# Four-layer decoder trunk: q, k and v of an attention head projected with time on partitions, and a scheduler with other durations

## The chip, the cores and the metric

The kernel runs on one core of a Trainium2 chip. The metric is device time in microseconds (us) of one execution. The kernel before was run three times: 1918.64, 1926.33 and 1927.67 us, a median of 1926.33. Its profile is of one further execution.

A core has five engines that matter here, each with a queue that it works through in order: TensorE (PE in the profile; its weight loads are PEld), VectorE (DVE), ScalarE (ACT), GpSimd (POOL) and SyncE (SP), which here only issues DMA transfers.

## The reference

x is 512 steps of time by D = 1024 channels. Four layers, each `x + Mixer(RMSNorm(x))`, with the mixers A, B, C, A; the inner width is E = 2048.

```python
def conformer_conv_mixer(h, ...):                     # A: layers 0 and 3
    val, glu_gate, z = jnp.split(h @ w_in, 3, axis=-1)
    u = causal_depthwise_conv(val * jax.nn.sigmoid(glu_gate), conv_w) + conv_b   # 31 taps
    u = jax.nn.silu(layer_norm(u, ln_g, ln_b))
    return (u * jax.nn.silu(z)) @ w_out

def forgetting_attention_mixer(h, ...):               # B: layer 1; 16 heads of 128 channels
    q, k, v, z, f_logit = jnp.split(h @ w_in, [E, 2 * E, 3 * E, 4 * E], axis=-1)
    q = rms_norm(q, q_norm_g); k = rms_norm(k, k_norm_g)        # per head
    c = jnp.cumsum(jax.nn.log_sigmoid(f_logit + f_bias), axis=1)
    # logits = q k^T / sqrt(128) + c[t] - c[s] for s <= t, softmax, times v
    o = blocked_forgetting_attention(q, k, v, c)
    return (o * jax.nn.silu(z)) @ w_out

def short_conv_mixer(h, ...):                         # C: layer 2
    u, b_gate, c_gate, z = jnp.split(h @ w_in, 4, axis=-1)
    return (b_gate * causal_depthwise_conv(c_gate * u, conv_w) * jax.nn.silu(z)) @ w_out
```

All of it is float32.

## The kernel before, in words

**Matrix products.** Channels lie on the 128 partitions and the 512 steps of time along the columns. Every operand of a product is cut into two parts of the type fp32r, `hi` (a cast) and `lo` (the rest, by a subtraction), and a product is three: hi·hi, hi·lo and lo·hi. The weights come in chunks of 128 x 1024 (512 KB) by DMA from SP into a ring of three places, `w_raw`; ACT casts a chunk to `w_hi` (L309), POOL or DVE makes `w_lo` (L407), each in a ring of four. One chunk gives 24 matmuls: 8 tiles of d, three products, 512 columns each (`project`). So each use of a chunk needs, in this order, its DMA, its cast on ACT and its subtraction.

**The order.** The code lists all operations in the order of the computation. `Plan.trace` then deals them out: it keeps an estimated duration for each operation and engine, and lets each engine that is free by these estimates take the first operation in the list whose operands are there. An operand counts as there LATENCY = 0.13 us after the end of the operation that made it. The chip never sees the estimates. It sees each engine's order, and semaphores for what must be waited for. A wrong estimate therefore gives an order in which an engine waits at one instruction while others behind it could run.

**A conformer layer.** The in-projection (val, gate, z) and the 31 taps run together, taps on DVE and POOL (a few tiles on PE). Then the layer norm, and sixteen tiles g, each made by DVE and ACT from a tile `d` and cut into `g_hi` (ACT, L309) and `g_lo` (DVE or POOL, L360). The out-projection (`out_projection`) takes them for 384 matmuls: accumulators o0 to o3 take two tiles g at a time, a pair with one chunk (24 matmuls, 8 pairs, 192 in all); o4 to o7 need all sixteen g and take two chunks each (48 matmuls each).

**Attention.** After f (the forget gates) there are sixteen heads. In each, q, k, v and z are projected by one chunk each into a bank of PSUM, channels on partitions, and multiplied by the layer's `rstd` on DVE (`take`, L324). The norms of q and k are over partitions: the squares are cut in two parts and summed by matmuls with a matrix of ones (`qs`, `ks`), and 1/sqrt is worked out on 128 x 512 (`rsqrt`). v is transposed on PE (`vt`). Logits `lg` for four blocks of 128 query steps have 128 to 512 columns; DVE adds the forget gates (`ct`, and `nc` from DMA) and the mask, ACT takes the exponential, DVE divides by `rsum`. The probabilities are transposed (`pt`, in the one bank `tr`), cut in two parts, and multiplied with v into `op`. In the second half of the heads their z·op products are cut into g as in a conformer layer, and the out-projection is the same.

PSUM has eight banks: three `mm`, two `acc`, and one each of `tr`, `sum` and `o`. A bank is taken again only when all that read it are done.

**Layer 2** has the same kind of projections without heads; its order comes from the same planner.

## Time and profile before

| | us |
|---|---|
| three runs | 1918.64, 1926.33, 1927.67 |
| span of the profiled execution, first to last instruction | 1925.0 |
| PE busy | 1789.5 |
| DVE busy | 1306.4 |
| POOL busy | 1030.9 |
| ACT busy | 903.1 |

The page gives no time of the profiled execution apart from its span, which lies 1.3 us under the median of the runs. The page cuts the span into 40 slices, of 48 us each:

```profile
PE   6999997799999998989999999999999899999789
DVE  7999999826777767687724344444412899989851
PEclk9999998899999999999999999999999999999889
```

The first row is PE's busy share in tenths, the second that of DVE, the third the TensorE clock that was granted. Layer 0 takes slices 1 to 9, attention 10 to 21 or so, layer 2 up to slice 31, and layer 3 the rest. The dips of PE stand near the end of the layers 0 and 3, together with dips of the clock.

### The profile page before, as it was taken

The page shows a single profiled execution, that of the slowest core. Times are in us where ns is not written, and L with a number is a line of the kernel's source. Part 1 is how long each engine was busy: PE and PEld are TensorE (multiplying, and loading weights), DVE is VectorE, ACT ScalarE, POOL GpSimd, SP SyncE. Part 2 cuts the span into 40 slices and gives each one's busy share as a digit, 9 for nine tenths or more (in the row PEclk, how much of TensorE's full clock was granted, in tenths as well). Part 3 has the DMA queues.
Part 4 walks back from the last instruction along what each step waited for, and adds up shares of the span by engine and source line. Part 5 has one row for each costly group of instructions (what it writes and reads, how often), then busy time and mean ns, then how long its engine had stood idle before and what let it go on. Part 6 is the DMA issues. An engine that isn't in the chain of part 4 may idle for free. (4 is left out here: it accounts for less than half of the span.)

```text
span 1925.0 us, 21354 instructions
## 1 busy us (share of the span) xinstructions
PE 1789.5 (93%) x7952; PEld 1454.9 (76%) x7952; DVE 1306.4 (68%) x1829; ACT 903.1 (47%) x1335; POOL 1030.9 (54%) x598
## 2 busy tenths in 40 slices
PE   6999997799999998989999999999999899999789
PEld 4788885587787777767778788888888677878567
DVE  7999999826777767687724344444412899989851
ACT  5567864335565555555523222222223456775531
POOL 6899785544344333443435332323334599967652
PEclk9999998899999999999999999999999999999889
DMA  4233321122322221212122223232322232322112
GB/s 165 98 122 101 124 93 55 55 88 89 105 82 83 71 73 64 83 44 66 66 77 92 94 93 105 88 109 88 103 95 88 88 132 88 113 96 88 58 63 77
DMA packets 51831, 171.36 MB, mean 89 GB/s; under 512 B 5888, under 2 KB 5888, under 8 KB 51728
## 3 DMA queue, kind: packets, MB, share of 16 engines
q1 hardware_dynamic: 51728, 170.01, 26.2%
q8 instruction: 62, 1.02, 0.2%
q14 instruction: 41, 0.34, 0.1%
HBM read 167.86 MB, written 2.13 MB: 88 GB/s over the span
## 5 line engine op out<-in xcount | busy, mean ns | idle before, releaser
L407 POOL TENSOR_TENSOR w_lo<-w_raw,w_hi 128x1024 fp32r<-128x1024 f32 x244 | 597.3, 2454 | 722.3 <-PE z L373 227.4
L309 ACT CAST w_hi<-w_raw 128x1024 fp32r<-128x1024 f32 x289 | 302.7, 1051 | 550.1 <-PE z L373 169.4
L335 DVE SCALAR_TENSOR_TENSOR cv<-u,vt,cv 128x487 f32<-128x487 f32 (+25 forms) x710 | 464.5, 728 | 2.0
L373 PE MATMUL o<-g_hi,w_hi 128*128 128x512 f32 x512 | 136.3, 409 | 43.8 <-ACT g_hi L309 23.1
L324 DVE TENSOR_TENSOR x<-o,x 128x512 f32<-128x512 f32 x32 | 20.9, 686 | 212.3 <-PE o L373 212.3
L373 PEld LDWEIGHTS o<-g_hi,w_hi 128*128 128x128 f32 x512 | 100.7, 198 | 68.2 <-ACT g_hi L309 24.6
L373 PE MATMUL o<-g_lo,w_hi 128*128 128x512 f32 x512 | 129.8, 395 | 5.9 <-DVE g_lo L360 5.9
L373 PE MATMUL o<-g_hi,w_lo 128*128 128x512 f32 x512 | 128.9, 393 | 0.0
L324 POOL TENSOR_TENSOR pacc<-prod,pacc 128x508 f32<-128x508 f32 (+3 forms) x104 | 124.5, 1202 | 7.9 <-ACT prod L311 5.5
L373 PEld LDWEIGHTS o<-g_lo,w_hi 128*128 128x128 f32 x512 | 97.2, 191 | 28.1 <-DVE g_lo L360 7.7
L373 PEld LDWEIGHTS o<-g_hi,w_lo 128*128 128x128 f32 x512 | 97.0, 190 | 20.3
L407 DVE TENSOR_TENSOR w_lo<-w_raw,w_hi 128x1024 fp32r<-128x1024 f32 x45 | 78.9, 1758 | 18.9 <-PE u L373 17.7
L243 ACT ACT_TABLE_LOAD x69 | 88.5, 1283 | 1.2
L311 ACT ACTIVATE prod<-u,vt 128x510 f32<-128x510 f32 (+4 forms) x124 | 79.8, 710 | 15.5 <-DVE u L324 15.4
L324 DVE TENSOR_TENSOR z<-z,rstd 128x512 f32<-128x512 f32 x32 | 22.1, 692 | 92.2 <-PE z L373 92.2
L373 PE MATMUL z<-hl,w_hi 128*128 128x512 f32 x256 | 73.0, 433 | 0.0
L373 PE MATMUL z<-hn_hi,w_hi 128*128 128x512 f32 x256 | 66.6, 405 | 5.1 <-ACT sz L311 4.5
L373 PE MATMUL val<-hn_hi,w_hi 128*128 128x512 f32 x224 | 58.2, 399 | 11.9 <-ACT hn_hi L309 6.1
L373 PE MATMUL z<-hh,w_lo 128*128 128x512 f32 x256 | 65.9, 400 | 3.4 <-DVE w_lo L407 3.4
L373 PE MATMUL z<-hn_hi,w_lo 128*128 128x512 f32 x256 | 64.5, 395 | 0.0
L373 PE MATMUL z<-hn_lo,w_hi 128*128 128x512 f32 x256 | 64.5, 395 | 0.0
L373 PE MATMUL z<-hh,w_hi 128*128 128x512 f32 x256 | 63.6, 391 | 0.8 <-DVE u L324 0.8
(247 smaller groups left out, 3902.6 us busy)
## 6 DMA issues: line engine op xcount, KB each, us to landing
w_raw<-w SPq DMA_DIRECT2D x289, 512.0 KB, 3.6
pw<-pw SPq DMA_DIRECT2D x36, 256.0 KB, 4.4
nc<-cd SPq DMA_DIRECT2D x16, 256.0 KB, 4.1
x<-x SPq DMA_DIRECT2D x8, 256.0 KB, 5.5
out<-x SPq DMA_DIRECT2D x8, 256.0 KB, 2.2
vt<-vec SPq DMA_DIRECT2D x1, 577.5 KB, 4.6
cd<-nc SPq DMA_DIRECT2D x1, 32.0 KB, 1.6
vt<-vec SPq DMA_DIRECT2D x1, 16.0 KB, 1.7
```

What stands on the lines that cost most here:

```text
L243: switch(table)
L309: nc.scalar.copy(of(dst, d), of(src, s))
L311: nc.scalar.activation(of(dst, d), of(src, s), func, **kw)
L324: eng[e].tensor_tensor(of(dst, d), of(a, s), of(b, sb), op)
L335: nc.vector.scalar_tensor_tensor(of(dst, d), of(a, s), c, bb.bitcast(F32) if b_f32r else bb, op0, op1)
L373: nc.tensor.matmul(o, a, b, start=start, stop=stop)
L407: eng[e].tensor_tensor(lo(), raw(), hi().bitcast(F32), A.subtract)
```

## The change

**1. Attention's projections.** For a head, q, k and v are computed together with time on the partitions. The stationary operand is a block of 128 time steps of the layer's input (`hh` or `hl`), the moving one holds the weights of q, k and v side by side, 384 columns. Four banks (three `mm` and `sum`) take the four blocks of time. The weights come in a new array `wq`, four chunks of 128 x 768 (384 KB) for a head, each with two tiles of d. That makes 96 matmuls of 384 columns a head. z keeps its form (`gate`) and goes to the bank `o`; `op` goes to `acc`. f has an array of its own, `wf`, with a chunk of 240 columns.

The norms are now sums along a row: ACT squares a block, DVE adds up the 128 columns of q and of k into a 128 x 8 tile, and 1/sqrt is worked out on 128 x 8. v is scaled straight out of the bank by ACT (`vh`) and DVE (`vl`), without a transpose; q and k are scaled on DVE (`qk`) and then transposed on PE (`across`, eight transposes a head). The layer's own 1/sqrt is needed per row as well (`norm_tokens`: eight small matmuls).

```diff
-        def take(h, name):
-            acc, f = psum("mm", f"{name}{h}"), slot(f"{name}{h}")
-            project(acc, h_)
-            tt(("dve",), f, acc, st.rstd, A.mult, boost=-200)
-            return f
-        def normalise(f, h, name, g):
-            sq = slot("sq")
-            act(sq, f, AF.Square)
-            sp = split(sq, "sq", ("dve", "pool"))
-            ms = psum("sum", f"{name}s{h}")
-            sums(ms, ones_hr, sp)
-            stt(f, f, g, rsqrt(ms, "r"), A.mult, A.mult)
-            return split(f, f"{name}{h}", ("dve", "pool"))
+        def tokens(h):
+            banks = [psum("mm" if b < 3 else "sum", f"qkv{h}_{b}") for b in range(NB)]
+            for c in range(ND // 2):
+                hi, lo = chunk()
+                for b in range(NB):
+                    ks = (2 * c, 2 * c + 1)
+                    mms(lambda b=b, ks=ks, hi=hi, lo=lo: [
+                            (banks[b]()[:, : 3 * HD], a[k]()[:, blk(b)],
+                             w()[:, (k - ks[0]) * 3 * HD : (k - ks[0] + 1) * 3 * HD],
+                             k == 0 and g == 0, k == ND - 1 and g == 2)
+                            for k in ks for g, (a, w) in enumerate(
+                                ((st.hh, hi), (st.hl, hi), (st.hh, lo)))],
+                        [banks[b]], 6 * pe_time(3 * HD),
+                        [hi, lo, *(a[k] for k in ks for a in (st.hh, st.hl))])
+            ssq, r, nt, rr = norms[h % 2]
+            for b in range(NB):
+                sq, s = slot("sq"), slice(0, 2 * HD)
+                act(sq, banks[b], AF.Square, s=s)
+                plan.op({"dve": dve_time(2 * HD)}, lambda e, b=b, sq=sq, s=s: nc.vector.tensor_reduce(
+                    ssq()[:, 2 * b : 2 * b + 2], sq()[:, s].rearrange("p (a c) -> p a c", c=HD),
+                    mybir.AxisListType.X, A.add), [sq], [ssq])
+            vh, vl = slot(f"vh{h}", F32R), slot(f"vl{h}", F32R)
+            for b in range(NB):
...
+            tt(("dve",), ssq, ssq, rt2, A.mult, s=n8)
+            rsqrt(ssq, None, bufs=(r, nt), s=n8)
+            tt(("dve",), rr, r, rt, A.mult, s=n8)
...
+                plan.op({"dve": dve_time(2 * HD)}, scale, [banks[b], rr], [qk[b // 2]])
+            return qk, vh, vl
+        def gate(h):
+            zp, z = psum("o", f"z{h}"), slot(f"z{h}")
+            project(zp, h_)
+            tt(("dve",), z, zp, st.rstd, A.mult)
+            act(z, z, AF.Silu)
+            return z
```

**2. Smaller edits in attention.** The mask is an `affine_select` on POOL in place of an addition on DVE. The `lo` parts of weights and of g are made by DVE alone in this layer.

```diff
-        lo_engines["now"] = ("pool", "dve")
+        lo_engines["now"] = ("dve",)
...
-                plan.op({"dve": 0.2}, lambda e, i=i: nc.vector.tensor_tensor(
-                    p[i]()[:, blk(i)], p[i]()[:, blk(i)], mask(), A.add), [p[i], mask], [p[i]])
+                plan.op({"pool": 0.3}, lambda e, i=i: nc.gpsimd.affine_select(
...
-            op = psum("o", f"op{h}")
+            op = psum("acc", f"op{h}")
...
-            gh[k], gl[k] = split(gs[k], f"g{layer}_{k}", ("dve", "pool"))
+            gh[k], gl[k] = split(gs[k], f"g{layer}_{k}", ("dve",))
```

**3. The planner's durations, for all layers.** They are set nearer to a trace, and an operand made by TensorE for another engine, or by another engine than one's own, counts as there later:

```diff
-    LATENCY = 0.13
+    LATENCY = 0.15
+    SLACK = 0.9
...
-                p.ready = max(p.ready, end + self.LATENCY)
+                late = 0.0
+                if len(p.engines) > 1 or e not in p.engines:
+                    late = self.LATENCY + (self.SLACK if "pe" in p.engines else 0.0)
+                p.ready = max(p.ready, end + late)
...
-        return 0.07 + n * (0.52e-3 if fast else 1.042e-3)
+        return 0.16 + n * (0.52e-3 if fast else 1.042e-3)
+    def pe_time(n):
+        return max(0.108, 0.0105 + n * 0.4225e-3)
...
-        t = 0.1 + 0.835e-3 * width(s)
+        t = 0.17 + 0.835e-3 * width(s)
...
-                        accs, 0.216 * half, [a, b[k]])
+                        accs, pe_time(T) * half, [a, b[k]])
...
-        act(hi, raw, None, cost=0.95, boost=-600)
-        cost = {"dve": 1.13, "pool": 2.3}
+        act(hi, raw, None, s=s, boost=-600)
+        cost = {"dve": dve_time(cols), "pool": 0.14 + 2.2e-3 * cols}
```

SLACK is added where the operation that waits (`p`) is TensorE's and its operand was made elsewhere. Within one engine nothing is added any more.

**What moves on the engines.** The rows give a line, an operation, its output and its inputs with running numbers, and the size. First TensorE in layer 0's out-projection, at the end of the fifth pair of g (g0_8, g0_9). Before:

```order
L373 MATMUL o0_324_2784<-g0_9_hi_346_2909,w_lo52_2848 128x512
L373 MATMUL o1_325_2785<-g0_9_hi_346_2909,w_lo52_2848 128x512
L373 MATMUL o2_326_2786<-g0_9_hi_346_2909,w_lo52_2848 128x512
L373 MATMUL o3_327_2787<-g0_9_hi_346_2909,w_lo52_2848 128x512
L373 MATMUL o4_371_3039<-g0_0_hi_328_2778,w_hi56_3033 128x512
L373 MATMUL o4_371_3039<-g0_1_hi_330_2782,w_hi56_3033 128x512
```

And of the change, in the same place:

```order
L401 MATMUL o2_323_2778<-g0_9_hi_343_2912,w_lo52_2833 128x512
L401 MATMUL o3_324_2779<-g0_9_hi_343_2912,w_lo52_2833 128x512
L401 MATMUL o0_321_2776<-g0_10_hi_345_2928,w_hi53_2874 128x512
L401 MATMUL o1_322_2777<-g0_10_hi_345_2928,w_hi53_2874 128x512
L401 MATMUL o2_323_2778<-g0_10_hi_345_2928,w_hi53_2874 128x512
```

Before, TensorE turned to o4 and chunk 56 after five pairs and mixed the other three pairs in behind; now it takes all eight pairs first, and o4 to o7 follow, 48 matmuls each.

The second place is ACT's queue for the same stretch, with the last tiles g and the cast of chunk 56. Before:

```order
L309 CAST g0_13_hi_354_2986<-d13_256_2425 128x512
L309 CAST w_hi55_2992<-w_raw55_2871 128x1024
L309 CAST g0_14_hi_356_3001<-d14_280_2685 128x512
L309 CAST g0_15_hi_358_3009<-d15_295_2737 128x512
L309 CAST w_hi56_3033<-w_raw56_2926 128x1024
```

Of the change:

```order
L337 CAST w_hi55_2972<-w_raw55_2859 128x1024
L337 CAST g0_12_hi_349_2981<-d12_243_2574 128x512
L339 ACTIVATE d13_253_2357<-d13_253_2357,vt_1_71 128x512
L339 ACTIVATE d14_277_2697<-d14_277_2697,vt_1_71 128x512
L339 ACTIVATE d15_292_2730<-d15_292_2730,vt_1_71 128x512
L337 CAST g0_13_hi_351_3011<-d13_253_2357 128x512
L337 CAST w_hi56_3017<-w_raw56_2902 128x1024
```

The cast of chunk 55 has moved ahead of g0_12 and that of chunk 56 ahead of g0_14; both still stand among the last tiles.

The third place is the border between two heads. TensorE of the change, behind the last matmul of z6 (pt5_1 and pt5_0 are the transposes of head 5's last probability blocks, qkv7_0 the first bank of head 7):

```order
L401 MATMUL z6_688_5504<-hh1_7_381_3428,w_lo99_5354 128x512
L904 MATMUL pt5_1_669_5559<-ident_14_81,p5_1_660_5424 128x128
L904 MATMUL pt5_1_669_5559<-ident_14_81,p5_2_658_5412 128x128
L904 MATMUL pt5_1_669_5559<-ident_14_81,p5_3_656_5390 128x128
L904 MATMUL pt5_0_672_5584<-ident_14_81,p5_0_662_5477 128x128
L904 MATMUL pt5_0_672_5584<-ident_14_81,p5_1_660_5424 128x128
L904 MATMUL pt5_0_672_5584<-ident_14_81,p5_2_658_5412 128x128
L904 MATMUL pt5_0_672_5584<-ident_14_81,p5_3_656_5390 128x128
L401 MATMUL qkv7_0_718_5598<-w_hi100_5384,hh1_0_357_3133 128x384
```

Before, the rest of v and eight matmuls of z stood between pt_1 and pt_0 (here of head 6):

```order
L373 MATMUL v7_779_5454<-hl1_7_385_3445,w_hi95_5270 128x512
L822 MATMUL pt6_1_751_5533<-ident_16_87,p6_1_742_5444 128x128
L822 MATMUL pt6_1_751_5533<-ident_16_87,p6_2_740_5415 128x128
L822 MATMUL pt6_1_751_5533<-ident_16_87,p6_3_738_5403 128x128
L373 MATMUL v7_779_5454<-hh1_0_360_3311,w_lo95_5300 128x512
...
L373 MATMUL z7_784_5565<-hh1_7_384_3441,w_hi96_5364 128x512
L822 MATMUL pt6_0_754_5577<-ident_16_87,p6_0_744_5448 128x128
```

The two transposes, which share the bank `tr`, were apart, with sixteen matmuls of v and z between them; now they follow each other at once, and the next head's first bank comes right behind. DVE of the change at the next border, from z7 to the scaling that empties head 7's first bank:

```order
L352 TENSOR_TENSOR z7_731_5874<-z7_730_5815,rstd1_411_3488 128x512
L440 TENSOR_TENSOR w_lo108_5878<-w_raw108_5721,w_hi108_5865 128x768
L388 TENSOR_TENSOR pt6_1_lo_713_5880<-pt6_1_711_5870,pt6_1_hi_712_5876 128x384
L833 SCALAR_TENSOR_TENSOR vl7_727_5854<-qkv7_1_719_5608,rt_414_3497,vh7_726_5834 128x128
L363 SCALAR_TENSOR_TENSOR nt_1_406_4011<-ssq_1_404_3936,r_1_405_3991 128x8
L363 SCALAR_TENSOR_TENSOR nt_1_406_4011<-nt_1_406_4011,r_1_405_3991 128x8
L363 SCALAR_TENSOR_TENSOR r_1_405_3991<-nt_1_406_4011,r_1_405_3991 128x8
L352 TENSOR_TENSOR rr_1_407_4018<-r_1_405_3991,rt_414_3497 128x8
L833 SCALAR_TENSOR_TENSOR vl7_727_5854<-qkv7_2_720_5634,rt_414_3497,vh7_726_5834 128x128
L844 TENSOR_TENSOR qk7_0_728_5900<-qkv7_0_718_5598,rr_1_407_4018 128x256
```

Of these rows only the first and the split of pt6_1 had a counterpart before; the others are new, and head 8's first matmul stands behind the last of them.

More of the change, by code (lines that the diff above doesn't have):

```diff
@@ L65, in in_order, with sequence @@
     if kind == "B":
-        return ["f"] + [n * NE + h for h in range(NE) for n in range(4)]
+        order = ["f"]
+        for h in range(NE):
+            order += [("qkv", h, c) for c in range(ND // 2)] + [3 * NE + h]
+        return order
     return [n * NE + i for i in range(NE) for n in (0, 2, 1, 3)]
-N_CHUNKS = sum(len(in_order(k)) + 16 for k in LAYERS)
+WF = ND * NE + P - NE
+WQ = 2 * 3 * HD
+def sequence():
+    count = {"w": 0, "wq": 0, "wf": 0}
+    out = []
+    for kind in LAYERS:
+        for n in in_order(kind) + [None] * 16:
+            name, cols = ("wf", WF) if n == "f" else ("wq", WQ) if isinstance(n, tuple) else ("w", 1024)
+            out.append((name, count[name], cols))
+            count[name] += 1
+    return out
+SEQ = sequence()
+N_CHUNKS = len(SEQ)
 LN_EXP = "natural_log_exp_and_others"
@@ L504, in norm, with norm_tokens @@
             self.rstd = rsqrt(ms, f"rstd{self.layer}", boost)
+        def norm_tokens(self):
+            nb = 2 * (T // P)
+            ms, s = psum("tr", "mst"), slice(0, nb)
+            plan.op({"pe": 0.9}, lambda e: [
+                nc.tensor.matmul(ms()[:, 2 * j : 2 * j + 2], a()[:, j * P : (j + 1) * P],
+                                 ones_d()[:, :2], start=n == 0, stop=n == 1)
+                for j in range(T // P) for n, a in enumerate((self.ssq, self.last))],
+                [self.ssq, self.last, ones_d], [ms])
+            return rsqrt(ms, None, bufs=(small("rt", nb), small("rt_nt", nb)), s=s)
         def normalise(self):
@@ L829, in head @@
                          for j in range(NB)],
-                [op], 1.75, [vh, vl, *(b for j in range(NB) for b in pt[j])])
+                [op], 1.9, [vh, vl, *(b for j in range(NB) for b in pt[j])])
             gs[h] = z
```

123 lines of the change are left out of this document (76 added, 47 removed).

## The prediction

> **What bounds the kernel now.** I read the page first, then busy time by stage, then the chain that ended last, then the timeline of TensorE at the largest holes.
>
> ```profile
> span 1925.0 us, 21354 instructions
> PE 1789.5 (93%) x7952; PEld 1454.9 (76%) x7952; DVE 1306.4 (68%) x1829; ACT 903.1 (47%) x1335; POOL 1030.9 (54%) x598
> ```
>
> TensorE (PE) is busy 93% of the span and nothing else is near. A shorter time needs fewer TensorE microseconds or fewer TensorE waits. The windows show where the waits are; the columns are the stretch, its length, then the busy time of PE, weight loads, VectorE (DVE), ScalarE (ACT) and GpSimd (POOL), the granted clock, the DMA share and GB/s.
>
> ```profile
> 330.00:437.00 107.00, 93.78 (x390) 75.95 (x389) 63.63 (x54) 42.14 (x58) 58.05 (x30) 0.92 0.20 66
> 437.00:960.00 523.00, 478.04 (x2204) 387.63 (x2202) 381.60 (x637) 289.03 (x490) 213.26 (x107) 0.97 0.23 76
> 960.00:1057.00 97.00, 94.71 (x425) 77.44 (x425) 33.59 (x46) 32.20 (x47) 42.03 (x20) 1.00 0.24 80
> 1057.00:1410.00 353.00, 350.85 (x1542) 288.85 (x1541) 152.80 (x180) 90.72 (x100) 117.17 (x53) 1.00 0.30 98
> 1497.00:1815.00 318.00, 292.82 (x1313) 236.82 (x1312) 298.36 (x422) 189.74 (x276) 247.09 (x162) 0.98 0.29 98
> 1815.00:1925.00 110.00, 93.64 (x384) 75.58 (x382) 47.99 (x48) 30.35 (x40) 49.31 (x23) 0.92 0.18 62
> ```
>
> The rows are: layer 0's out-projection, attention's heads, attention's out-projection, layer 2, layer 3's convolution, layer 3's out-projection. Layer 2 is full (350.85 of 353): an order cannot help there. The convolution of a conformer layer is filled by DVE (298.36 of 318) with taps that the change leaves alone. The two conformer out-projections lose 13 and 16 us and run at a clock of 0.92; the heads lose 45. Only these places can give much.
>
> **Step 1: the new durations, in the conformer out-projections.** The chain, and the timelines of PE, ACT and DVE (start, length, instruction, idle time before and its releaser):
>
> ```profile
> 1859.16 62.26 PE o L373 x264
> ```
> ```profile
> 329.49 3.78 PE L373 MATMUL o<-g_hi,w_hi 128*128 128x512 f32 x8 [13.51 <-ACT g_hi L309]
> ```
> ```profile
> 373.13 5.49 PE L373 MATMUL o<-g_hi,w_hi 128*128 128x512 f32 x12 [10.66 <-ACT w_hi L309]
> ```
> ```profile
> 984.66 1.98 PE L373 MATMUL o<-g_hi,w_hi 128*128 128x512 f32 x8
> 986.47 1.98 PE L373 MATMUL o<-g_lo,w_hi 128*128 128x512 f32 x8
> ```
> ```profile
> 371.00 1.13 ACT L309 CAST g_hi<-d 128x512 fp32r<-128x512 f32 x2
> 372.04 1.04 ACT L309 CAST w_hi<-w_raw 128x1024 fp32r<-128x1024 f32 x1
> ```
> ```profile
> 371.60 1.21 DVE L407 TENSOR_TENSOR w_lo<-w_raw,w_hi 128x1024 fp32r<-128x1024 f32 x1
> 372.74 3.45 DVE L360 TENSOR_TENSOR g_lo<-d,g_hi 128x512 fp32r<-128x512 f32 x2
> ```
> ```profile
> 1857.58 4.66 DVE L360 TENSOR_TENSOR g_lo<-d,g_hi 128x512 fp32r<-128x512 f32 x4
> ```
>
> Eight matmuls of 512 columns take 986.47 − 984.66 = 1.81 us, so one is **0.2266 us**. An out-projection has 384: 192 for its first four accumulators (o0 to o3, with g as it comes) and 48 for each of o4 to o7. The old order has TensorE do five of the eight pairs of g (120), then turn to o4. That needs the cast of weight chunk 56, which stands behind three late g casts in ACT's queue (371.00, 372.04). So TensorE waits 10.66 us, and 264 matmuls are still to come when it resumes: 62.26 us in layer 3, where they are the whole chain.
>
> In the new order TensorE takes all eight pairs for o0 to o3 and only then o4 to o7. The same DVE and ACT work precedes the last g, so I leave the end of its split where it is: 372.74 + 3.45 = 376.2 in layer 0, 1857.58 + 4.66 = 1862.2 in layer 3. At that point the last pair's share (12 matmuls, 2.7 us) and 192 others (43.5 us) are left, 46.2 us. The ends come at 422.4 instead of about 437.0 (where the window ends), and 1908.4 instead of 1859.16 + 62.26 = 1921.4: gains of **14.6 and 13.0, together 27.6**. Before that point 180 matmuls (40.8 us) must fit into the 46.7 us from 329.49 to 376.2; they do, though with little to spare. The upper bound is 32, with the last g coming 2 us sooner in each layer, about the length of the second split in a row like 372.74. The lower bound is 0: PE is in order, and if the g come unevenly it waits at each of them instead of once.
>
> **Step 2: attention's heads.** The prices first: logits' matmuls of 384 columns, transposes, DVE's groups over the heads, and the marks of the heads.
>
> ```profile
> 761.94 0.33 PE L373 MATMUL lg<-k_hi,q_hi 128*128 128x384 f32 x1
> 762.11 0.34 PE L373 MATMUL lg<-k_lo,q_hi 128*128 128x384 f32 x1
> ```
> ```profile
> 439.54 0.50 PE L373 MATMUL f<-hh,w_hi 128*128 128x512 f32 x1 [1.16 <-ACT hh L311]
> ...
> 475.22 0.39 PE L373 MATMUL lg<-k_hi,q_hi 128*128 128x512 f32 x1
> ...
> 482.61 0.60 PE L791 MATMUL vt<-ident,v 128*128 128x128 f32 x4
> 482.96 0.47 PE L373 MATMUL qs<-sq_lo,ones_hr 128*128 128x512 f32 x1
> ...
> 964.38 0.51 PE L373 MATMUL lg<-k_hi,q_hi 128*128 128x512 f32 x1 [0.38 <-ACT k_hi L309]
> ```
> ```profile
> L324 DVE TENSOR_TENSOR z<-z,rstd 128x512 f32<-128x512 f32 x16 | 11.1, 692 | 14.7 <-PE z L373 14.6
> L360 DVE TENSOR_TENSOR pt_lo<-pt,pt_hi 128x384 fp32r<-128x384 f32 x15 | 8.2, 546 | 0.0
> L814 DVE RECIPROCAL rsum<-rsum 128x1 f32<-128x1 f32 x60 | 8.2, 153 | 2.2 <-ACT p L311 2.1
> L335 DVE SCALAR_TENSOR_TENSOR p<-lg,ct,nc 128x128 f32<-128x128 f32 x15 | 5.1, 341 | 0.0
> ```
>
> *TensorE's work.* The first logits of heads 0 and 15 are 489.2 us apart: **32.6 us a head**. By prices the old head is 96 × 0.2266 = 21.75 (q, k, v, z), 4 sums 0.9, 14 transposes at 0.35 for four (482.61 to 482.96) 1.2, logits and output of 3840 columns each at 0.000453 a column 1.75 + 1.75: 27.4, so 5.2 is waiting, slow clock and refilling. The new one is 96 × 0.174 (762.11 − 761.94, rounded up) = 16.7 for q, k, v, z 24 × 0.2266 = 5.4, no sums, 18 transposes 1.6, logits and output 3.5: 27.2, and 0.7 for four breaks of the stream (a lone matmul lasts 0.33, not 0.174): 27.9. The rewrite itself thus saves TensorE next to nothing: fewer columns a matmul, but just as many of them.
>
> *The new wait.* Behind the last z matmul of a head TensorE has the transposes of the last two probability blocks, in one bank after each other, then q, k, v of the next head, whose first bank must first be emptied. DVE empties it at the end of its own queue: z × rstd 0.69, the 768-column weight split 0.91 (three quarters of 1.21, row 371.60), the split of pt1 0.55, a v split 0.34 (row of 128 columns), four row-sum operations of 8 columns 4 × 0.16 (row of 153 ns), another v split 0.34, the scaling of q and k 0.42 (256 columns, between the 128 and 384 rows). That is 3.9, and 0.2 until DVE sees the matmul: 4.1. The seven transposes (0.65) lie beside it, so TensorE waits **3.4 us**, and a head is 27.9 + 3.4 = 31.3. The wait is bounded by 0 (DVE takes the other six before z arrives) and by 4.1 × 1758/1210 = 6.0 (DVE as slow as its mean weight split in the page, 1758 ns); I take the quiet price, since POOL has next to nothing left to do in the heads. ACT ends as late: a table load, SiLU of z, two v scalings.
>
> *Start and end.* From the first f matmul to the first logits it was 35.7 us. Now: f 5.4, sums 1.9, q, k, v of head 0 16.7, z 5.4, half of the next q, k, v 8.4, transposes 1.3, a wait of 3.3 for the norms and 1.3 for a table: 43.7. From the last head's logits to 1057 it was 92.6; of this 352 matmuls of the out-projection (79.8), and logits, transposes and output (5.0) stay, 84.8, the last head's projections being finished before its logits. So 35.7 + 489.2 + 92.6 = 617.5 becomes 43.7 + 15 × 31.3 + 84.8 = 598.0. The 16 splits of g are all DVE's now (16 × 0.69 = 11) and fall among the heads; I charge 8, with bounds of 0 and 11. **Gain 11.5.** Mask additions go to POOL, which is idle there; queues on SP carry the same bytes a head (four loads of 384 KB and one of 512 against four of 512): nothing for either. In layer 2 and the convolutions the order moves without a place to gain: 0, ± 3.
>
> **Sum.** 1925.0 − 27.6 − 11.5 = 1885.9 for the profiled execution. The median of the runs shown is 1926.3, 1.3 above its span, so I forecast **1887**.
>
> **The clock after a wait.** The trace has both outcomes:
>
> ```profile
> 814.41 0.63 PE L822 MATMUL pt<-ident,p 128*128 128x128 f32 x4 [2.22 <-DVE pt_lo L360]
> ...
> 815.11 3.08 PE L373 MATMUL z<-hl,w_hi 128*128 128x512 f32 x8
> ...
> 838.40 0.30 PE L822 MATMUL pt<-ident,p 128*128 128x128 f32 x1 [1.72 <-DVE rsum L814]
> 838.45 2.10 PE L373 MATMUL k<-hl,w_hi 128*128 128x512 f32 x8
> ```
>
> After 2.22 us of idle eight matmuls took 3.08, after 1.72 they took 2.10. The new wait of 3.4 is cut in two by the transposes of the last block, about 2.0 and 1.4, so it lies at the edge. The sum has no charge for it. The Trainium skill, page "TensorE: Matmul & The Clock Gate", section "What's actually happening", lets the clock fall only after a whole window of some 3.4 us without work; by that rule neither piece costs clock and 1887 stands. The trace speaks against the rule as a safe bound, since 2.22 us was enough here (a trailing slow stretch from another cause would look the same).
>
> **The rivals.**
> - *Each head's wait halves the clock* (0.17): 1.0 to 1.5 us a head, from the rows above, 15 × 1.5 = 22: **1909**.
> - *The order brings nothing* (0.12; the change then doesn't do what its numbers are for): TensorE, now in step with g, waits at each pair for ACT and DVE, and the last g comes late by what was to be gained, since w_hi casts stand nearer to g casts. 1887 + 27.6 = **1915**, at the edge of no change.
> - *Slower* (0.08): 96 matmuls of 384 columns with new stationary data each don't run at 0.174, because loading those data sets the pace. The logits show 0.174 for three in a row only; the load rows of the page have means near 0.19 (beside matmuls of 0.2266, so nothing pressed them). Transposes at 0.35 for four, each with a load, speak against it. At 0.2266 it costs 96 × 0.053 × 16 = 81: 1968. It decides from 1936 on, that is at 0.206 us a matmul.
> - *Better* (0.08): DVE does the row sums before z, and the wait shrinks to 2: 15 × 1.4 = 21 less, **1866**.
> - The rest (0.05) is small losses that meet: within 0.5%.
>
> One more rule would change a term:
>
> ```profile
> 758.00 1.28 ACT L243 ACT_TABLE_LOAD   x1
> 759.29 0.63 ACT L311 ACTIVATE z<-z 128x512 f32<-128x512 f32 x1
> ```
>
> Here the activation starts 0.01 us after the load has ended. The Trainium skill, page "ScalarE: Activation LUTs", section "What ACT_TABLE_LOAD costs", adds a drain of about 1.4 us to each switch; by it ACT's branch would end some 1.1 us after DVE's in each head, 15 × 1.1 = 17, an estimate of 1904. This row shows no such drain.
>
> **How the numbers follow.** A measurement of this kernel can tell about 0.5%: faster is under 1916.7, slower over 1936. The forecast (1875 to 1900) has 0.50; faster also holds the clock, the better case and a third of the order's failing: 0.79. The other two thirds and the rest make same 0.13; slower 0.08. The range takes in 1866 and 1915 with 4 and 6 beyond for the ± 3 and the g splits: 1862 to 1921.
>
> **What would show it.** In the new profile the two out-projections should have no wait near 10 us at o4 and should last 10 to 15 us less; q, k, v matmuls should come 0.174 apart; after each head's z two waits of TensorE near 2.0 and 1.4 should stand, released by DVE; first logits should be 31.3 apart. The forecast is wrong if g comes later than before, if q, k, v are paced by loads, or if the granted clock in the heads falls below 0.95.

## The result, and the profile after

The changed kernel takes 1954.16 us (median of four runs, 1953.31 to 1957.01), against 1924.78 for the kernel before, measured beside it: a ratio of 1.0159, 95% interval 1.0138 to 1.0180. It is slower, by 1.6%, where the prediction had it faster. (One kernel among the experiments ran at two speeds, 1906.7 us at a granted clock of 0.963 in three executions and 1878.07 at 0.983 in one, so it has no ratio.) The page after:

```profile
span 1952.5 us, 22370 instructions
PE 1786.7 (92%) x8352; PEld 1510.1 (77%) x8352; DVE 1290.1 (66%) x1927; ACT 872.0 (45%) x1369; POOL 857.9 (44%) x565
...
PE   6999997599898989899899999999999999989289
...
DVE  7999999973565656567644334333403999999991
...
PEclk9999998699999999999999999999999999999699
```

The totals hardly differ from before: TensorE has 3 us less to do and still ends 27.5 us later, so it waits 30 us more. The slices say where: PE's 5 in slice 8 and its 2 in slice 38 (counted from 1) stand in the two conformer layers, each with a dip of the clock, and DVE is at 9 up to there. The windows, cut at the first out-projection matmul and the first mean-square matmul of each layer (columns as before):

```profile
329.36:365.29 35.93, 7.57 (x8) 2.35 (x8) 31.68 (x41) 8.00 (x11) 7.94 (x5) 0.55 0.01 2
365.29:465.52 100.23, 94.09 (x391) 76.47 (x392) 66.37 (x57) 43.07 (x61) 58.45 (x31) 0.95 0.21 70
465.52:1073.20 607.68, 562.08 (x3025) 514.51 (x3024) 363.26 (x804) 293.76 (x573) 38.55 (x71) 0.98 0.24 79
1073.20:1503.80 430.60, 430.27 (x1894) 355.45 (x1893) 149.34 (x165) 113.18 (x130) 215.49 (x102) 1.00 0.28 97
1503.80:1851.53 347.73, 300.66 (x1344) 243.83 (x1342) 321.46 (x423) 189.48 (x276) 244.08 (x160) 0.94 0.26 90
1851.53:1952.50 100.97, 91.86 (x384) 74.45 (x384) 53.75 (x47) 31.19 (x41) 47.39 (x24) 0.96 0.20 68
```

The first row is new: before, layer 0's out-projection began at 329.49. Now DVE works on for 35.93 us, with 41 instructions, while TensorE has eight matmuls to do. The same marks in both traces:

| stretch | before | after | difference |
|---|---|---|---|
| start and convolution, layer 0 | 329.5 | 365.3 | +35.8 |
| out-projection, layer 0 | 107.9 | 100.2 | -7.6 |
| attention | 619.6 | 607.7 | -11.9 |
| layer 2 | 440.0 | 430.6 | -9.4 |
| convolution, layer 3 | 317.4 | 347.7 | +30.3 |
| out-projection, layer 3 | 110.6 | 101.0 | -9.6 |
| span | 1925.0 | 1952.5 | +27.5 |

Part of the -9.4 is work handed on: layer 2 has 32 matmuls fewer (1926 before, 1894 now) and the convolution behind it 31 more, some 7 us of TensorE's time. What grew are the convolutions. DVE's timeline in a stretch of taps (each tap multiplies a tile by one weight of the convolution and adds to an accumulator `cv`), first before, then after:

```profile
149.38 8.37 DVE L335 SCALAR_TENSOR_TENSOR cv<-u,vt,cv 128x500 f32<-128x500 f32 x13
```
```profile
149.45 12.25 DVE L363 SCALAR_TENSOR_TENSOR cv<-u,vt,cv 128x497 f32<-128x497 f32 x16
```

13 taps in 8.37 us are 0.64 each; 16 in 12.25 are 0.77. The taps are the same. Their order isn't. DVE's rows before and after (output tile first):

```order
L335 SCALAR_TENSOR_TENSOR cv0_1_94_485<-u_88_421,vt_1_71,cv0_1_94_485 128x484
L335 SCALAR_TENSOR_TENSOR cv0_2_106_702<-u_100_500,vt_1_71,cv0_2_106_702 128x502
L335 SCALAR_TENSOR_TENSOR cv0_1_94_485<-u_88_421,vt_1_71,cv0_1_94_485 128x483
L335 SCALAR_TENSOR_TENSOR cv0_2_106_702<-u_100_500,vt_1_71,cv0_2_106_702 128x501
L335 SCALAR_TENSOR_TENSOR cv0_1_94_485<-u_88_421,vt_1_71,cv0_1_94_485 128x482
```
```order
L363 SCALAR_TENSOR_TENSOR cv0_2_103_784<-u_97_496,vt_1_71,cv0_2_103_784 128x505
L363 SCALAR_TENSOR_TENSOR cv0_2_103_784<-u_97_496,vt_1_71,cv0_2_103_784 128x504
L352 TENSOR_TENSOR u_134_810<-val0_5_131_684,sg_133_805 128x512
L363 SCALAR_TENSOR_TENSOR cv0_2_103_784<-u_97_496,vt_1_71,cv0_2_103_784 128x503
L363 SCALAR_TENSOR_TENSOR cv0_2_103_784<-u_97_496,vt_1_71,cv0_2_103_784 128x502
```

Before, the taps of two tiles alternate; now those of one tile follow each other. Of 738 instructions that write a `cv`, 56 stood right behind one of the same accumulator before, and 680 do now. The old planner had a result count as there 0.13 us after its instruction, on its own engine too, and so took another tile's tap in between. The new one adds nothing within an engine. The groups of taps over the whole program (count, then busy us and mean ns of one record, then idle time ahead of them), before and after:

```profile
L335 DVE SCALAR_TENSOR_TENSOR cv<-u,vt,cv 128x487 f32<-128x487 f32 (+25 forms) x710 | 464.5, 728 | 2.0
```
```profile
L363 DVE SCALAR_TENSOR_TENSOR cv<-u,vt,cv 128x499 f32<-128x499 f32 (+25 forms) x710 | 523.2, 737 | 24.1
```

The records are nearly equally long, 728 and 737 ns. But 710 x 728 would be 517 us: before, neighbours overlapped by 0.07 us on average. The new ones do not overlap, and have 24 us of idle time ahead of them. Busy and idle together, the group grew by 80.8 us.

### The profile page after: what moved, and what is told of

It is laid out like the page before. It is cut to its first block, busy times and chain, and to the rows that moved or that the text cites. A ratio compares the mean times of both kernels' runs of the same rounds, so it can differ in the third digit from the quotient of the medians.

```text
span 1952.5 us, 22370 instructions
## 1 busy us (share of the span) xinstructions
PE 1786.7 (92%) x8352; PEld 1510.1 (77%) x8352; DVE 1290.1 (66%) x1927; ACT 872.0 (45%) x1369; POOL 857.9 (44%) x565
## 4 chain that ended last, share of the span: by engine, by line
PE 59%; DVE 35%; ACT 4%; issue 2%; DMA 0%; POOL 0%; SPq 0%; DVEq 0%; ACTq 0%; POOLq 0%
DVE cv L363 26%; PE o L401 15%; PE qkv L401 14%; PE z L401 9%; PE c L401 4%; PE u L401 4%; PE b L401 4%; DVE d L352 3%; PE op L401 2%; PE lg L401 2%; DVE g_lo L388 1%; DVE u L352 1%; ACT L267 1%; ACT pt_hi L337 1%; ACT phases L653 1%
## 5 line engine op out<-in xcount | busy, mean ns | idle before, releaser
L440 POOL TENSOR_TENSOR w_lo<-w_raw,w_hi 128x1024 fp32r<-128x1024 f32 (+1 forms) x204 | 492.1, 2413 | 369.6 <-ACT w_hi L337 82.4
L337 ACT CAST w_hi<-w_raw 128x1024 fp32r<-128x1024 f32 (+1 forms) x305 | 305.6, 1003 | 602.9 <-PE z L401 129.4
L363 DVE SCALAR_TENSOR_TENSOR cv<-u,vt,cv 128x499 f32<-128x499 f32 (+25 forms) x710 | 523.2, 737 | 24.1
L401 PE MATMUL qkv<-w_hi,hh 128*128 128x384 f32 x512 | 180.8, 353 | 18.1 <-ACT pt_hi L337 14.9
L401 PE MATMUL qkv<-w_lo,hh 128*128 128x384 f32 x512 | 174.5, 341 | 0.0
L401 PE MATMUL qkv<-w_hi,hl 128*128 128x384 f32 x512 | 174.5, 341 | 0.0
L440 DVE TENSOR_TENSOR w_lo<-w_raw,w_hi 128x768 fp32r<-128x768 f32 (+1 forms) x101 | 107.8, 1068 | 80.2 <-ACT w_hi L337 50.4
L401 PEld LDWEIGHTS o<-g_hi,w_hi 128*128 128x128 f32 x512 | 98.3, 193 | 49.2 <-ACT g_hi L337 27.5
L352 POOL TENSOR_TENSOR pacc<-prod,pacc 128x510 f32<-128x510 f32 (+1 forms) x104 | 125.0, 1202 | 14.6 <-ACT prod L339 10.3
L401 PEld LDWEIGHTS qkv<-w_hi,hl 128*128 128x128 f32 x512 | 98.3, 192 | 0.2 <-DVE hl L363 0.2
L401 PEld LDWEIGHTS qkv<-w_lo,hh 128*128 128x128 f32 x512 | 98.0, 191 | 0.0
```

Of the source, the lines that this page charges most:

```text
L337: nc.scalar.copy(of(dst, d), of(src, s))
L352: eng[e].tensor_tensor(of(dst, d), of(a, s), of(b, sb), op)
L363: nc.vector.scalar_tensor_tensor(of(dst, d), of(a, s), c, bb.bitcast(F32) if b_f32r else bb, op0, op1)
L401: nc.tensor.matmul(o, a, b, start=start, stop=stop)
L440: eng[e].tensor_tensor(lo()[:, s], raw()[:, s], hi()[:, s].bitcast(F32), A.subtract)
```

## The experiments

The theory at first: the taps of one accumulator in a row are the whole loss. Three kernels and a measurement of taps by themselves:

**Latency within an engine, put back into the changed kernel.**

```diff
-                late = 0.0
+                late = self.LATENCY
                 if len(p.engines) > 1 or e not in p.engines:
```

> The changed kernel, with the 0.15 us of latency kept between instructions of one engine as well. Theory (the planner, seeing no latency within DVE, lays the taps of one accumulator behind each other, and each such tap waits for the one before): the taps of two tiles alternate again, a tap takes about 0.65 us instead of 0.77, layer 0's out-projection starts at 330 +- 6 us instead of 365, layer 3's convolution shrinks by about 30, and the whole takes 1952.5 - 66 = 1886 +- 10 us. Rival (the convolutions are longer because of the new durations, which change who makes w_lo and when POOL works, or because of attention's new form): within 10 us of 1952.

Measured: 1956.87 us, ratio to before 1.0175 (1.0134 to 1.0215). The taps alternate again and cost what they did (463.6 us busy), yet the whole is no faster than the change. Layer 0's convolution is 346.1 us, between the two; layer 3's is 323.5. But attention is back at 617.8, layer 2 at 445.5, and layer 0's out-projection at 107.8. So latency 0 within an engine has a good side as well, and the convolution of layer 0 has a second cause. As a forecast of the time the theory failed.

**The reverse: the kernel before, without latency within an engine.**

```diff
-                p.ready = max(p.ready, end + self.LATENCY)
+                late = self.LATENCY if len(p.engines) > 1 or e not in p.engines else 0.0
+                p.ready = max(p.ready, end + late)
```

> The kernel before, with the latency left out between instructions of one engine, all else as before. Theory: the taps of one accumulator follow each other, each convolution takes 30 to 36 us longer, and the whole is 1925 + 66 = 1991 +- 12 us. Rival (durations or attention): within 10 us of 1925.

Measured: 1954.92 us, ratio 1.0151 (1.0120 to 1.0182). The convolutions go to 361.3 and 343.8 (+31.8 and +26.4) and the tap group reads 523.2 us and 24.1 idle, to the digit as in the changed kernel. This one line makes nearly all of the convolutions' loss, 58 of 66 us. The forecast of 1991 missed the other side: out-projections -8.9 and -6.8, attention (in its old form) -8.1, layer 2 -10.9. In the out-projections and in layer 2 that is about what the change gained.

**The new attention with the old planner.** The latency and the durations of before; edits 1 and 2 of the change stay.

```diff
-                late = 0.0
-                if len(p.engines) > 1 or e not in p.engines:
-                    late = self.LATENCY + (self.SLACK if "pe" in p.engines else 0.0)
+                late = self.LATENCY
...
-        return 0.16 + n * (0.52e-3 if fast else 1.042e-3)
+        return 0.07 + n * (0.52e-3 if fast else 1.042e-3)
...
-        t = 0.17 + 0.835e-3 * width(s)
+        t = 0.1 + 0.835e-3 * width(s)
```

> The changed kernel's attention with the planner's latency and durations of before (new operations keep their own). Theory: the convolutions are as before (first out-projection matmul of layer 0 at 330 +- 4), the out-projections of layers 0 and 3 again wait near 10 us once, attention gives its 12 us (from 619 to 607): 1925 - 12 = 1913 +- 8. Rival (the new attention's operations push the convolutions): over 1935.

Measured: 1871.59 us, ratio 0.9724 (0.9697 to 0.9751). Convolutions 328.0 and 318.3, out-projections 107.1 and 111.4, as expected, but attention takes 562.2 us by the marks of the table, not 607. The new form is worth 57 us; the new planner gives 45 of them back. (Several expectations below take 569 or 570 us for this run's attention, and so a loss of 28 or 38 us. That value runs to 1004.23, where a later mean-square matmul of layer 2 starts; the first one starts at 997.27.) TensorE's waits in the heads of the changed kernel, and of this one (who waits for whom, us in total, times, longest):

```profile
PE pt L904 <- DVE pt_lo L388: 26.0, 15, 1.8
PE qkv L401 <- ACT pt_hi L337: 14.9, 14, 1.1
```
```profile
PE qt L864 <- DVE qk L842: 2.8, 2, 2.5
PE qkv L399 <- DVE qk L842: 1.6, 1, 1.6
```

The two waits of each head, 41 us in all, are a matter of the order alone: the operations are the same.

**Taps by themselves.** Rows of 60 taps on DVE in one, two or three accumulators, with nothing else running.

```python
for i in range(60):
    t = tiles[i % len(tiles)]
    nc.vector.scalar_tensor_tensor(t[:, T - cols :], u[:, :cols], wt[:, i : i + 1],
                                   t[:, T - cols :], A.mult, A.add)
```

> Only a row of taps on DVE and copies of x: 60 taps of 500 columns in one accumulator in PSUM, 60 alternating between two, 60 between three, then the same in SBUF with one and two, then 128 columns with one and two. It computes nothing of the reference. Theory: in one accumulator a tap starts 0.75 to 0.78 us after the one before, with two or three 0.63 to 0.66; the difference of 0.12 us is a fixed time for each instruction, so it is there with 128 columns too. Rival (DVE is slower in the changed kernel because ACT and POOL load its ports): one, two and three agree within 0.02 us.

Groups (count | busy us, mean ns | idle time ahead):

```profile
L269 DVE SCALAR_TENSOR_TENSOR one<-u,wt,one 128x500 f32<-128x500 f32 x60 | 44.6, 744 | 3.9 <-DMA u<-x 1.8
L269 DVE SCALAR_TENSOR_TENSOR sone<-u,wt,sone 128x500 f32<-128x500 f32 x60 | 44.4, 740 | 2.1
L269 DVE SCALAR_TENSOR_TENSOR stwo<-u,wt,stwo 128x500 f32<-128x500 f32 x60 | 39.0, 732 | 0.0
L269 DVE SCALAR_TENSOR_TENSOR three<-u,wt,three 128x500 f32<-128x500 f32 x60 | 38.7, 738 | 0.0
L269 DVE SCALAR_TENSOR_TENSOR two<-u,wt,two 128x500 f32<-128x500 f32 x60 | 38.7, 737 | 0.0
...
L269 DVE SCALAR_TENSOR_TENSOR alone<-u,wt,alone 128x128 f32<-128x128 f32 x60 | 21.1, 352 | 2.1
L269 DVE SCALAR_TENSOR_TENSOR pair<-u,wt,pair 128x128 f32<-128x128 f32 x60 | 15.7, 345 | 0.0
```

In one accumulator a tap takes (44.6 + 2.1) / 60 = 0.78 us, in two or three 38.7 / 60 = 0.645. The difference of 0.13 us is there in SBUF and in PSUM, and with 128 columns too ((21.1 + 2.1) / 60 = 0.39 against 0.26). So for a tap it is a fixed price of reading what the instruction before it wrote, and the rival is out. In the kernel 624 more such pairs (680 less 56) times 0.133 are 83 us of DVE time, near the 80.8 by which the group of taps grew. The convolutions are 66 us longer; why not by all 81 stays open.

The theory then had three causes: taps in a row; a tap planned too long (the new estimate takes 0.74 us, the length of its record, though alternating taps start 0.645 apart, so DVE would be ahead of the plan and meet operands that aren't there); and SLACK, for the heads.

**Latency between taps alone**, in the changed kernel. Taps are marked, and only a pair of them keeps it.

```diff
-                late = 0.0
+                late = self.LATENCY if o.tap and p.tap else 0.0
```

> The changed kernel, with the 0.15 us of latency kept only between two taps of a convolution. Theory of three causes (1: taps of one accumulator in a row; 2: a tap is planned at 0.74 us, the length of its record, though interleaved taps start every 0.64 us, so DVE runs ahead of the plan and waits for ACT and PE; 3: SLACK of 0.9 us puts two transposes at the end of each head). This run takes away cause 1 alone: the convolutions come to what they were with the latency kept everywhere (346 and 323 us), the rest stays as in the changed kernel: 1952.5 - 19 - 24 = 1909 +- 8 us. Rival (the latency within PE, ACT or POOL matters to the convolution too): a convolution of layer 0 still over 355.

Measured: 1906.79 us, ratio 0.9908 (0.9880 to 0.9936). Convolutions 342.4 and 319.9, all else as in the changed kernel (attention 607.6, layer 2 430.6). The first cause is worth 22.9 + 27.8 = 51 us. DVE's waits up to layer 0's out-projection show the second:

```profile
DVE u L353 <- ACT sg L340: 13.7, 11, 2.2
```

Eleven times DVE stands at `u` waiting for ACT's sigmoid; the kernel before has one such wait, of 2.3 us. The changed kernel has one too, of 0.8 us: this cause shows only once the taps alternate and DVE is faster than its plan.

**Shorter taps in the plan besides.**

```diff
-        t = dve_time(width(s)) + (0.06 if isinstance(scalar, tuple) else 0)
+        t = dve_time(width(s)) + (0.06 if isinstance(scalar, tuple) else 0) - (0.09 if tap else 0)
```

> The changed kernel, with the latency kept between taps and a tap planned 0.09 us shorter, near the 0.64 us at which interleaved taps start. Theory: causes 1 and 2 gone, both convolutions as before the change (329 and 318 us, +- 4), the rest as in the changed kernel: 1952.5 - 66 = 1887 +- 8 us. Rival (the planned length of a tap doesn't matter; the excess of layer 0 has another cause, like SLACK between the projections and what DVE and ACT do with them): layer 0's convolution stays at 340 to 350, the whole at 1905.

Measured: layer 0's convolution 327.7 us, layer 3's 309.2; the waits at `u` are down to this:

```profile
DVE u L353 <- ACT sg L340: 1.9, 2, 1.2
```

The second cause is worth 14.7 + 10.7 = 25 us by this, and the rival is out. The profile is of an execution of 1906.63 us, whose extra time lies in attention (634.1 us, against 607.6 in the run before); the convolutions of the run of all three causes below take 330.0 and 309.9, which makes it 22 us. Layer 3's came out below the range expected.

**SLACK at 0 in the changed kernel**, nothing else.

```diff
-    SLACK = 0.9
+    SLACK = 0.0
```

> The changed kernel with SLACK at 0, all else as in it. Theory: of the three causes it takes away the third; pt_1 and pt_0 are again apart in TensorE's order, the two waits of each head (41 us in all) go, attention takes 570 +- 6 us instead of 608, the convolutions stay at 365 and 348: 1952.5 - 38 = 1914 +- 8 us. Rival (attention is slower because of the durations or of the latency within an engine): attention stays over 600, the whole over 1940.

Measured: 1953.63 us, ratio 1.0152 (1.0130 to 1.0173). Attention takes 597.9 us: 10 less, where 38 were expected. Eight matmuls of z now stand between pt_1 and pt_0, but the two waits of a head are still there, the second under another name:

```profile
PE pt L904 <- DVE pt_lo L388: 23.6, 14, 1.9
PE qkv L401 <- DVE qk L844: 11.7, 13, 0.9
```

The third cause as stated fell: SLACK is a small part of it.

**All three causes removed.** Latency between taps, shorter taps, SLACK 0: the three diffs above together.

> The kernel of the run before this one (latency between taps, shorter taps), and SLACK at 0 besides. Theory: all three causes gone, the out-projections, layer 2 and attention's projections keep what they gained: 1887 - 38 = 1849 +- 10 us, faster than all others so far. Rival (SLACK is what gave the gain in the out-projections and in layer 2): those stretches go back to 108, 440 and 110, and the whole is about 1870.

Measured: 1877.70 us, ratio 0.9756 (0.9737 to 0.9774). The out-projections (99.5 and 106.7) and layer 2 (430.6) keep their gains without SLACK, so that rival is out, but attention stays at 599.3 and the whole is 29 us over the forecast. What was left open is why the heads cost 37 us more than with the old planner: the latency within an engine, or the durations.

**The changed kernel with latency kept everywhere and SLACK 0**, which then differs from the run of attention alone by the durations (and by a LATENCY of 0.15 in place of 0.13): the first diff of these experiments and the one of SLACK together.

> The changed kernel with SLACK 0 and the 0.15 us of latency within an engine as well: it differs from the run of attention alone by the durations. Theory (the durations cost the heads the other 28 us): attention 595 to 600 us, layer 2 near 440, out-projections near 107, taps alternate but planned too long, so layer 0's convolution is 340 to 350. Rival (latency 0 within an engine costs the heads): attention 570 +- 6.

Measured: 1956.73 us, ratio 1.0163 (1.0125 to 1.0201). Attention 592.6 against 562.2: the durations, 30 us. The remaining stretches are worse than expected (356.3, 114.1, 447.7, 332.7, 112.1).

**Old durations, no latency within an engine but between taps**, on the new attention. To the run of attention alone:

```diff
                 late = self.LATENCY
+                if len(p.engines) == 1 and e in p.engines and not (o.tap and p.tap):
+                    late = 0.0
```

> The new attention with the durations and the latency of before, but no latency between instructions of one engine, except between taps. Theory (the two gains and the two losses are separate: latency 0 within an engine gives the out-projections and layer 2 their gain, latency between taps keeps the convolution, the old durations keep the heads as in the run with attention alone): convolutions 328 and 318, out-projections 100 and 104, attention 569, layer 2 431: 1850 +- 6 us. Rival (latency 0 within an engine is what costs attention its 28 us): attention 595 to 600, the whole 1877.

Measured: 1837.46 us, ratio 0.9541 (0.9520 to 0.9562). Stretches: 331.7, 97.6, 559.2, 429.1, 314.7, 101.5. Latency 0 costs the heads nothing, and each stretch keeps its gain. The time came out 7 us under the range expected, which added up an attention of 569 and a layer 2 of 431; with the table's mark, 562, the sum is 1843, and the forecast holds.

**New durations in the conformer layers only.** To the run before:

```diff
     def conformer(layer, st):
+        base.update(dve=0.16, act=0.17, pool=2.2e-3)
...
     def attention(layer, st):
+        base.update(dve=0.07, act=0.1, pool=2.11e-3)
```

> As the run before, with the new durations of DVE, ACT and POOL in the conformer layers only (a tap planned as before). Theory (the new durations help the convolution once taps are planned at their real distance: layer 3's took 309 us with them and 318 without): layer 3's convolution 309 to 312, the rest as in the run before: 1842 +- 6 us. Rival (those 9 us came from what stood ahead of the layer): no difference beyond 3 us.

Measured: 1850.31 us, ratio 0.9605 (0.9578 to 0.9632), 13 us slower than the run before. Layer 3's convolution is 314.2 against 314.7: no gain. Layer 0's out-projection went from 97.6 to 102.8, layer 3's from 101.5 to 105.8. So the theory fell. What gave the 309 us of the earlier runs stays open; it isn't DVE's constant, since the next run has 310.7 without it.

**One constant.** The run of all three causes removed, with DVE's constant back at 0.07 us, and every other new duration kept (a tap is planned as in that run, where it had 0.09 less than 0.16).

```diff
-        return 0.16 + n * (0.52e-3 if fast else 1.042e-3)
+        return 0.07 + n * (0.52e-3 if fast else 1.042e-3)
```

> The run of all three causes (latency between taps, SLACK 0), with the constant of every DVE estimate at 0.07 us, as before, in place of 0.16 (a tap is then no special case); ACT, POOL and TensorE keep the new durations. Theory (the 0.09 us by which records of neighbours on DVE overlap, counted twice by the new estimates, is what costs the heads the remaining 30 us): attention 564 to 572 us and no wait of pt for pt_lo near 1.7 us a head; the whole 1877 - 30 = 1847 +- 8 us. Rival (ACT's durations, or the longer exponential, cost the heads): attention stays at 592 to 600, the whole at 1877.

Measured: **1826.64 us, ratio 0.9473 (0.9453 to 0.9493)**, faster than both kernels and all other runs. Attention takes 555.9 us, 43 less than with the constant of 0.16. Its page, and all that TensorE waits for in the heads:

```profile
span 1825.0 us, 22361 instructions
PE 1762.6 (97%) x8352; PEld 1493.2 (82%) x8352; DVE 1222.4 (67%) x1930; ACT 873.9 (48%) x1369; POOL 845.9 (46%) x562
```
```profile
PE qt L867 <- DVE qk L845: 1.5, 2, 1.1
```

41 us of waits in the changed kernel's heads have become 1.5. TensorE's timelines show what moved. With the constant of 0.16 a head ends with sixteen matmuls of z, pt_1, eight of z and pt_0, and TensorE waits 1.7 us at pt_0 and 0.9 at the next head's first bank. With 0.07 only eight of z stand ahead of pt_0; the other sixteen, and op, stand behind it and fill the time. As for why: a head has some 47 DVE instructions (705 in the changed kernel's heads, over 15), so with 0.09 us too much on each the plan thinks DVE 4 us a head slower than it is, and places what waits for DVE that much later. This last step is an estimate and was not tested by itself.

## Why the prediction was wrong

**The step that failed.** The prediction said of the convolutions that DVE fills them "with taps that the change leaves alone", and of them and layer 2 that "the order moves without a place to gain: 0, ± 3". The term was +66 us (35.8 and 30.3). The taps are left alone in number and size, not in order, and the order of an engine that is full does have a price: 0.13 us for each tap that follows one on its own accumulator. The stage was rightly read as bound by DVE. The diff says that nothing is added within one engine any more (by itself this line costs the kernel before 58 us there), but in the conformer layers only TensorE's and ACT's orders were followed through it, not that of the engine which bounds the stage. No rival had this, so the range missed as well. Without the 66 us the changed kernel would stand at 1952.5 - 66.1 = 1886.4, beside a forecast sum of 1885.9. That agreement is luck in part: the out-projections gave 10.4 us less than forecast, and layer 2 9.4 that the sum had at 0.

**The conformer out-projections** (forecast -14.6 and -13.0, measured -7.6 and -9.6). The mechanism was right: the wait of 10.66 us at o4 is gone and o0 to o3 go in step with g. The size was off, since the sum let the last g decide. The changed kernel's chain reads otherwise:

```profile
405.01 59.04 PE o L401 x252
```

The wait that binds in layer 0 is at the sixth pair's g_lo, 39.7 us after the first matmul; from there 252 matmuls run without a stop, and 252 x 0.2266 is already 57 us. In the old trace the reader could see g come unevenly (waits of 1.61 and 0.95 us in the second and fourth pairs); the sum used one point of it.

**Attention** (forecast -11.5, measured -11.9 by the table). Here the steps held for the most part. From the first matmul of f to the first logits it took 44.3 us (43.7 forecast), the first logits are 31.9 apart on average (31.3), the end took 86.6 (84.8). The prediction's 35.7 us of before start at f's eighth matmul, though, at 439.54; the first is at 424.88. From the eighth it is 40.8 now, so the start grew by 5.1 us and not by 8.0. And the size of the whole is luck in part: 8 us were charged for the splits of g, fifteen of which fall between 856 and 981 us, and the first logits there are no further apart than elsewhere (29.6 to 32.2 us). Five other heads ran slower for a while, for which the sum charged nothing, and took as much (5 x 1.6 = 8). The two waits behind z stand where they were put:

```profile
719.79 0.66 PE L904 MATMUL pt<-ident,p 128*128 128x128 f32 x4 [1.79 <-DVE pt_lo L388]
721.58 0.41 PE L401 MATMUL qkv<-w_hi,hh 128*128 128x384 f32 x1 [1.13 <-ACT pt_hi L337]
```

1.8 and 1.1 us, where 2.0 and 1.4 were forecast. DVE releases the first. The second is put down to ACT's pt_hi, which ended last, at 721.45; but the matmul doesn't read it. What it needs is its bank, which DVE's scaling `qk` had emptied at 721.43, and with SLACK at 0 the same wait is put down to `qk`. So both are DVE's, as predicted. And TensorE's own work of 27.9 us a head is what is left once the waits are gone: in the last experiment the logits of all heads but the last are 28.0 to 28.2 apart. What the prediction didn't ask is whether the wait belongs to the new form or to the new numbers. It belongs to the numbers: with the old planner the same form has 4.4 us of waits in all heads.

**Layer 2** was called full, and it was: 430.27 of 430.60 us busy now. Its -9.4 is mostly work handed to the next stretch, where TensorE has room: with old durations and no latency but between taps, layer 2 takes 429.1 us and layer 3's convolution is no longer for it (314.7, against 317.4 before).

**The rivals.** "The order brings nothing" was nearest in kind, since numbers meant to fit the trace better made the order worse, but in another place and with another sign. "Slower" by the pace of weight loads is out: 90 of the first head's matmuls run at 15.71 / 90 = 0.1746 us,

```profile
474.07 15.71 PE qkv L401 x90
```

against 0.174 in the sum. The clock after the waits was a real rival, if a small one here: heads of the changed kernel are 31.4 or 33.0 us apart, with the same two waits. The 1.6 us between them is near the 1.0 to 1.5 foreseen, but it strikes five heads of fifteen. "Better" didn't come: the row sums still stand behind z, at 719.92 to 720.67 in the head above. Nor did the longer branch on ACT, at 1904: in the changed kernel too the activation of z starts 0.02 us after a table load (558.31 + 1.28 = 559.59, then 559.61).

## What to carry to other kernels

When a scheduler's numbers change, compare the order of the engine that bounds each stage first, row by row, and count how many instructions now follow one that they depend on. A duration taken from a trace is the length of a record; what a plan needs is the distance from one start to the next, apart for dependent and independent neighbours. And several numbers that all come "from the trace" can have opposite signs: here one line (no latency within an engine) was worth some 35 us of gain and 58 of loss in the kernel before, and the best kernel takes it everywhere but between taps.

## What the runs showed of the hardware

- On DVE a tap that reads what the instruction before it wrote starts 0.13 us later than an independent one: 0.78 against 0.645 us at 500 columns, in PSUM and SBUF alike, and 0.39 against 0.26 at 128. Independent neighbours' records overlap by 0.09 us (737 ns of record every 645). The Trainium skill, page "VectorE: DVE Perf Modes", section "The DRAIN you can't avoid", reports the same time for eight copies in a row with a semaphore after each as with one after the last alone: "the semaphore costs nothing extra here". No run here tests that sentence: every tap depends on an earlier one, the alternating ones too, and what costs 0.13 us is that the earlier one is the one right before.
- Waits of 1.8 and 1.1 us, with 0.66 us of transposes between them, came ahead of a slow stretch of TensorE in some heads and not in others. The first matmul behind them takes 0.66 us in one head of the changed kernel and 0.41 in another:

```profile
528.44 0.66 PE L401 MATMUL qkv<-w_hi,hh 128*128 128x384 f32 x1 [1.13 <-ACT pt_hi L337]
```
```profile
594.37 0.41 PE L401 MATMUL qkv<-w_hi,hh 128*128 128x384 f32 x1 [1.13 <-ACT pt_hi L337]
```

In the 3.2 us behind the first row the granted clock is 0.50 and the matmuls start 0.32 us apart, behind the second it is 1.00 and they start 0.17 apart. The slow stretch can start later, too: in the head of 561.36 the first matmul takes 0.41 us as well, and the slow stretch starts at the sixth. In the last experiment, whose heads have no such waits, all but one are 28.0 to 28.2 us apart.

The Trainium skill, page "TensorE: Matmul & The Clock Gate", section "What's actually happening", has the gate watch a window that runs freely and close only after a whole one of about 3.4 us without work. That the same wait has two outcomes agrees with a window which isn't tied to the program. That it closes at all after 1.8 and 1.1 us does not agree with a whole idle window, and the measurement decides: a pair of waits well under 3.4 us can cost the clock.
